# A hybrid decoder layer on one core: the mLSTM memory multiplied at the end, and two decoded rows on shared partitions

## The chip, the core and the metric

The kernel runs on one core of one Trainium2 chip. A core has a matrix engine (PE, with a second track PEld for the loading of its stationary operand), a vector engine (DVE), a scalar engine (ACT), a general engine (POOL) and a queue engine (SP) that issues transfers. ACT and POOL issue transfers as well. SBUF is the core's working memory with 128 partitions; PSUM holds what the matmuls write, in banks of 512 columns of float32.

The metric is the device time of one launch in microseconds, as a median over runs. All times are in microseconds (us) unless marked ns.

## What is computed

One layer of a hybrid decoder is applied to a prompt of 256 tokens and, in the same launch, to 8 single tokens that are being decoded (8 sequences, one new token each). The kernel puts them side by side as 264 columns. In terms of the reference:

```
x = x + W_out[ RGLRU-group(xn) || mLSTM-group(xn) ],  xn = RMSNorm(x)
x = x + CrossAttn(RMSNorm(x), memory K/V)   (4 heads, 256 memory tokens, no mask)
x = x + SwiGLU(RMSNorm(x))
y = RMSNorm_final(x)
```

Two parts matter here.

The mLSTM group has 4 heads with keys of 128 and values of 256. Beside its output, the layer must return each head's memory after the prompt. With the prompt starting from nothing it is one product over the 256 tokens, with a weight `w_end` for each token; the normaliser is the same product with a value of one:

```
C_new = dec[..., None, None] * C + jnp.einsum('bhs,bhsd,bhsv->bhdv', w_end, kc, vc)
n_new = dec[..., None] * n + jnp.einsum('bhs,bhsd->bhd', w_end, kc)
```

Nothing in the layer reads this memory again: it goes to an output (o_pc) and no further.

The cross attention of the 8 decoded rows reads cached keys and values of its own for each row and head, 256 tokens by 512:

```
s = jnp.einsum('blhd,bmhd->bhlm', xq, mk) * (XA_DH ** -0.5)
p = jax.nn.softmax(s, axis=-1)
o = jnp.einsum('bhlm,bmhd->blhd', p, mv)
```

There are 32 such (head, row) pairs, each with 512 KB of keys and 512 KB of values that are used once.

## The kernel before

Activations lie with the feature on the partitions: a [2048, 264] matrix is 16 chunks of [128, 264]. Every weight matrix is cut into pieces of 128 output features by up to 16 input chunks, and the list `steps` holds them in order: w_in (41 pieces), w_out (16), w_q (16), then w_k and w_v for each of the four heads (8 pieces a head), w_o (16), gate and up in three parts, each followed by its w_down pieces. For float32 precision each weight piece is split into a high part (ACT copies it to float32r) and a low part (DVE subtracts), and a product is three matmuls: high by high, high by low, low by high (`mm3`). SP loads the pieces three steps ahead (`load_piece`, line 176) into five buffers `raw`; they are split one step ahead (`split_half`) into four buffers `w`.

The main loop walks over `steps`: it evacuates the step before, splits the next piece, issues the matmuls of this one, loads a later one, and then calls `pump`. Everything that is not a weight matmul is written as a generator (`side`): the recurrent group, the mLSTM group (`ml_prompt`, `ml_values`, `ml_heads`, `ml_sample`, `ml_norm`), the memory's norm (`mem_gen`), the prompt's attention (`attend`), and the decoded rows' attention (`dec_k`, `dec_v`). `pump` runs the generators by their priority until modelled clocks of DVE and ACT have reached PE's, so side work is spread into what DVE and ACT have left in each step. A planner then fixes each engine's order by priorities and a modelled timeline. SP alone keeps the order in which the code is written. Each engine carries out its instructions in order, so one that waits holds up all behind it; POOL's arithmetic and the transfers that it issues are one such order. Nearly all instructions go through a helper and show as line 60 in the profile, so they are told apart by the names of their tiles.

Tiles named B are 26 buffers of about 4 KB per partition that nearly everything in flight shares. PSUM has four banks named mm, for weight matmuls, and four named ax.

The mLSTM heads (`ml_heads`). For head h, `kw` holds the keys times the weight `w_end` with the token on the partitions, two blocks of [128 tokens, 128]; `vt` holds the values with the ones beside them, two blocks of [128, 258]. Two float32 matmuls give the memory in a bank `cps`, ACT copies it into `cn`, and after the fourth head POOL issues one transfer of `cn` to `o_pc` (line 826). Each float32 matmul is two instructions in the profile.

The decoded rows' attention. `dec_k` takes a row: POOL loads keys `kc` (line 1151) and values `vc` (line 1155), each [128, 4, 256]: 512 features on 128 partitions in 4 chunks, by 256 tokens. The scores are summed over the chunks with ACT (first chunk times the query, a column of `qsm`) and DVE (three more multiply-adds) into `acc`, a part of the tile `dw`. ACT and POOL (line 1162) split `acc` into the high and low part `ds`, and in `dec_v` two float32r matmuls with a matrix of ones, `onesr`, sum over the partitions and leave the sum on all of them. DVE takes the maximum, ACT the exponential with its sum in `ssm`, and DVE multiplies each of the 4 chunks of values by the probabilities and sums over the tokens into a column of `osm`. After 8 rows of a head `osm` is divided by `ssm`, and `attend(h)` copies it beside the prompt's columns as input of w_o. At most `NFL` = 2 rows are between `dec_k` and the end of `dec_v`.

The end. In the last part of w_down, `final(m)` adds a piece's result to `xres`, adds its squares to `acc_x`, and scales by the gain into `y`. For the last piece (m = 15) the sum of squares is finished on PE (`fin_sums`), and `rstd_fin` makes the reciprocal root on DVE and ACT and spreads it over partitions by matmuls with `ident`, once into the bank `fin["ps"]` that DVE reads and once into `fin["copied"]`, which ACT copies to `rstd` for POOL. Between these, `warm` issues matmuls whose result nobody reads. Then DVE, and POOL for 4 of the 16 chunks, multiply `y`, and SP and ACT issue nine transfers to `o_y` (line 1495).

## Time and profile before

| | us |
|---|---|
| median of 3 runs | 1456.94 (1456.13 to 1457.64) |
| the profiled execution, own time | 1455.83 |
| its span, first to last instruction | 1454.1 |
| PE busy | 1439.2 (99%) |
| DVE busy | 1045.1 (72%) |
| ACT busy | 794.9 (55%) |
| POOL busy | 128.3 (9%) |
| transfers, mean | 224 GB/s |

The profiled execution is 1.1 below the median, and 1.7 of its time lies outside the span. A line of the groups reads: source line, engine, operation, names written and read, shapes, count, then the busy time of all, the mean ns of one, and the time that the engine sat idle just before them with what ended it. A line of the timeline begins with the start and the length of a merged stretch, both in us. Matmuls are pipelined: the length of one is from its start to its last result, while the next one starts much earlier, so the price of a matmul in a dense row is the distance from its start to the next start. The views by windows give the busy time of each engine in a stretch, then the granted clock of PE, the share of time for which the 16 transfer engines were busy, and the rate.

### The profile page before, as it was taken

Reading aid. Unit: us, or ns where it says so; the run is one execution under the profiler, and the core shown is the slowest. Engines: PE = TensorE matmul, PEld = TensorE weight load, DVE = VectorE, ACT = ScalarE, POOL = GpSimd, SP = SyncE. Lnnn points to the kernel's source line nnn. Section 1 sums busy time; section 2 is a strip of 40 time slices with the busy share of each in tenths; the row PEclk is TensorE's granted clock in tenths of the full one; section 3 lists DMA queues with packets and bytes.
Section 4 is the critical chain, followed back from the end, with each engine's and each line's share of the span. In section 5 each row is a group of like instructions: output and inputs, shape, how many; then the busy total and the mean of one; then the engine's idle time right before and its main releaser. Section 6 shows DMA issues by size and latency. Waiting matters only on the chain.

```text
span 1454.1 us, 30126 instructions
## 1 busy us (share of the span) xinstructions
PE 1439.2 (99%) x12071; PEld 1415.5 (97%) x12071; DVE 1045.1 (72%) x1999; ACT 794.9 (55%) x1279; POOL 128.3 (9%) x204
## 2 busy tenths in 40 slices
PE   9999999999999999999999999999999999999997
PEld 8999999999999999999999999999999999999997
DVE  7966797898899999987675666555665655565564
ACT  7678685666556666655544444434444443444463
POOL 0001210000124343410000000000000000000000
PEclk9999999999999999999999999999999999999999
DMA  9645896557799877955555555555555555555563
GB/s 288 234 171 179 268 363 231 177 178 271 254 344 355 340 284 297 375 172 192 197 195 194 197 193 201 190 202 190 198 194 196 196 198 194 195 197 192 172 195 112
DMA packets 99757, 326.02 MB, mean 224 GB/s; under 512 B 10944, under 2 KB 19824, under 8 KB 99616
## 3 DMA queue, kind: packets, MB, share of 16 engines
q1 hardware_dynamic: 83616, 269.84, 52.8%
q0 software_dynamic: 15136, 53.16, 10.2%
q8 instruction: 94, 1.54, 0.4%
q10 hardware_dynamic: 864, 1.09, 0.2%
q14 instruction: 47, 0.39, 0.1%
HBM read 312.78 MB, written 11.28 MB: 223 GB/s over the span
## 4 chain that ended last, share of the span: by engine, by line
PE 94%; ACT 2%; DMA 1%; DVE 1%; issue 1%; SPq 0%; POOL 0%; DVEq 0%; POOLq 0%
PE mm L60 90%; PE ax L60 5%; DMA raw<-w_in 1%; ACT B L60 1%; DVE B L60 1%; DMA B<-scr 0%; ACT w L60 0%; DVE w L60 0%; ACT L60 0%; SPq L213 0%; ACT dw L60 0%; DVE ds L60 0%; SPq L1412 0%; DMA scr<-lt 0%; ACT t L60 0%
## 5 line engine op out<-in xcount | busy, mean ns | idle before, releaser
L60 PE MATMUL mm<-B,w 128*128 128x264 f32 (+1 forms) x10960 | 1281.2, 279 | 2.5 <-DVE w L60 2.1
L60 PEld LDWEIGHTS mm<-B,w 128*128 128x128 f32 x10960 | 1260.6, 189 | 10.7 <-DVE w L60 2.4
L60 DVE TENSOR_TENSOR w<-raw,w 128x1024 fp32r<-128x1024 f32 (+1 forms) x522 | 625.4, 1200 | 312.9 <-ACT w L60 312.2
L60 ACT ACTIVATE w<-raw 128x1024 fp32r<-128x1024 f32 (+1 forms) x522 | 536.0, 1028 | 531.8 <-PE mm L60 370.8
L60 PE MATMUL mm<-w,B 128*128 128x512 f32 x384 | 86.5, 380 | 0.0
L60 PEld LDWEIGHTS mm<-w,B 128*128 128x128 f32 x384 | 70.7, 189 | 9.4
L1494 POOL TENSOR_TENSOR B<-B,rstd 128x264 f32<-128x264 f32 x4 | 2.8, 741 | 802.8 <-ACT rstd L60 802.8
L60 DVE TENSOR_TENSOR t<-mm,rstd 128x264 f32<-128x264 f32 x96 | 41.4, 432 | 28.8 <-PE mm L60 28.7
L60 DVE SCALAR_TENSOR_TENSOR B<-B,dw 128x256 f32<-128x256 f32 x128 | 52.2, 461 | 3.2 <-ACT dw L60 2.9
L60 DVE TENSOR_TENSOR xres<-xres,mm 128x264 f32<-128x264 f32 (+1 forms) x81 | 34.2, 424 | 27.2 <-PE mm L60 27.1
L60 DVE SCALAR_TENSOR_TENSOR dw<-B,qsm,dw 128x256 f32<-128x256 f32 x96 | 48.6, 512 | 0.8
L60 PE MATMUL ax<-B,B 128*128 128x256 f32 (+3 forms) x288 | 46.0, 302 | 0.8 <-DVE B L60 0.8
L1162 POOL TENSOR_TENSOR ds<-dw,ds 128x256 fp32r<-128x256 f32 x32 | 36.8, 1151 | 106.9 <-ACT ds L60 104.7
L60 PEld LDWEIGHTS ax<-B,B 128*128 128x128 f32 x288 | 39.9, 191 | 3.0 <-DVE B L60 1.0
L60 ACT ACTIVATE B<-xres,vecs 128x264 fp32r<-128x264 f32 (+1 forms) x64 | 32.1, 502 | 3.5 <-DVE xres L60 1.6
L60 ACT ACTIVATE t<-xres 128x264 f32<-128x264 f32 (+1 forms) x53 | 21.0, 409 | 16.0 <-DVE xres L60 16.0
L1151 POOL DMA_DIRECT2D B<-kcT x32 | 17.4, 544 | 122.8 <-DVE B L60 109.7
L60 DVE SCALAR_TENSOR_TENSOR B<-xres,vecs,B 128x264 fp32r<-128x264 f32 x48 | 23.3, 488 | 4.3 <-ACT B L60 4.3
L60 ACT ACTIVATE dw<-B,qsm 128x256 f32<-128x256 f32 x32 | 16.2, 507 | 16.3 <-issue 6.4
L60 ACT ACTIVATE B<-t 128x264 fp32r<-128x264 f32 (+1 forms) x60 | 24.1, 409 | 1.7 <-DVE t L60 1.5
L60 ACT ACTIVATE dw<-B,B 128x128 f32<-128x128 f32 x64 | 20.9, 390 | 7.1 <-DMA B<-scr 6.3
L60 ACT ACTIVATE dw<-ax,dw 128x256 f32<-128x256 f32 x32 | 15.0, 470 | 17.7 <-DVE dw L60 14.0
(172 smaller groups left out, 691.2 us busy)
## 6 DMA issues: line engine op xcount, KB each, us to landing
raw<-w_gu SPq DMA_DIRECT2D x176, 512.0 KB, 3.6
raw<-w_d SPq DMA_DIRECT2D x80, 512.0 KB, 3.7
raw<-w_in SPq DMA_DIRECT2D x74, 512.0 KB, 5.2
raw<-w_out SPq DMA_DIRECT2D x32, 512.0 KB, 3.8
B<-kcT POOLq DMA_DIRECT2D x32, 512.0 KB, 8.2
raw<-w_q SPq DMA_DIRECT2D x32, 512.0 KB, 5.4
B<-vcT POOLq DMA_DIRECT2D x32, 512.0 KB, 9.1
raw<-w_k SPq DMA_DIRECT2D x32, 512.0 KB, 5.1
```

The costliest lines, as they stand in the source:

```text
L60: return f(*a, **k)
L1151: pool_e.dma_start(kc, kcT[h, b])
L1162: pool_e.tensor_sub(ws[:, 1], acc, ws[:, 0].bitcast(F32))
L1494: e.tensor_mul(st["y"](c), st["y"](c), r)
```

## The change

Three things are changed.

First, `ml_heads` no longer multiplies the memory. It writes `kw` and `vt` of each head to DRAM (`kept_k`, `kept_v`; two transfers on POOL's queue a head), and the transfer of `cn` there is gone. In the last part of w_down, at m = 4, `state_load` reads them back on SP's queue into B tiles (`kb` for the keys, two `vb` for the values). The eight float32 matmuls are issued at the end on PE: one in place of two of three `warm` matmuls at m = 15, two in place of the three in `rstd_fin`, one behind the two spreads, and four behind that. ACT copies each head's bank out (`state_out`), and two transfers on SP's queue take the result to `o_pc`: heads 0 and 1 ahead of a transfer of `o_y`, heads 2 and 3 behind the last one. PE keeps the written order in the last step.

Second, the decoded rows' attention takes two rows of one head at once: one on partitions 0 to 63, the other on 64 to 127. A row's 512 features are then 8 chunks of 64. `onesr` becomes block diagonal, so that one pair of matmuls sums both rows apart. Because a row's query and result lie on all 128 partitions elsewhere, `swap_q` brings half of each row's query to the other half of the partitions (POOL copies and two transfers), and `swap_o` brings the results back.

Third, keys and values come through a `Ring` each: two fixed tiles, a tile being half of the features of both rows, filled by two transfers of 64 partitions (256 KB each) and filled again when the four instructions that read it are done.

```diff
@@ -442,11 +442,17 @@
...
         dve.scalar_tensor_tensor(r, t, 1.5, r, op0=OP.add, op1=OP.mult)
-        warm(3, v[:, 0:1])
+        state_mm((0, 1), (1, 0))
         for k in "ps", "copied":
...
             spread(fin[k], [r[:, j: j + 1] for j in range(3)])
+        state_mm((1, 1))
         act.activation(rstd, fin["copied"][:, :N], AF.Copy)
+        state_out(0, act)
+        state_out(1, act)
+        state_mm((2, 0), (2, 1), (3, 0), (3, 1))
+        state_out(2, act)
+        state_out(3, act)
...
@@ -737,6 +743,29 @@
...
     hT = {}
+    kept_k = drm.tile([H, P, T], F32, name="kept_k")
+    kept_v = drm.tile([H, P, 2, 258], F32, name="kept_v")
+    def state_load():
+        kb, vb, out = B([P, H, T]), [B([P, 2, 2, 258]), B([P, 2, 2, 258])], B([P, H, 258])
+        for h in range(H):
+            sp.dma_start(kb[:, h], kept_k[h])
+            sp.dma_start(vb[h // 2][:, h % 2], kept_v[h])
+        fin["state"] = kb, vb, out
+        fin["cps"] = {}
+    def state_mm(*parts):
+        kb, vb, out = fin["state"]
+        for h, t in parts:
+            if t == 0:
+                fin["cps"][h] = bank("ax" if h % 2 else "mm")
+            pe.matmul(fin["cps"][h][:, 0:258], kb[:, h, t * P: t * P + P], vb[h // 2][:, h % 2, t, :],
+                      start=t == 0, stop=t == 1)
+    def state_out(h, engine):
+        out = fin["state"][2]
+        engine.activation(out[:, h, :], fin["cps"][h][:, 0:258], AF.Copy)
...
@@ -796,7 +825,6 @@
...
     def ml_heads():
-        cn = B([P, H, 258])
         hT["t"] = Arr(8)
...
@@ -812,18 +840,15 @@
...
                           start=False, stop=True)
-            cps = bank("ax")
-            pe.matmul(cps[:, 0:258], kw[:, 0:P], vt[:, 0, :], start=True, stop=False)
-            pe.matmul(cps[:, 0:258], kw[:, P:T], vt[:, 1, :], start=False, stop=True)
-            dps = cps[:, 300:302]
+            pool_e.dma_start(kept_k[h], kw)
+            pool_e.dma_start(kept_v[h], vt)
+            dps = bank("ax")[:, 0:2]
             pe.matmul(dps[:, 0:1], Pm[:, 0:P], one, start=True, stop=True)
...
             act.activation(den[:, 3 * h: 3 * h + 2], dps, AF.Abs)
-            act.activation(cn[:, h, :], cps[:, 0:258], AF.Copy)
-        pool_e.dma_start(o_pc, cn)
         yield STEP
...
@@ -1036,7 +1061,8 @@
...
             else:
-                warm(3)
+                state_mm((0, 0))
+                warm(1)
                 sq = tmp()
...
@@ -1047,6 +1073,8 @@
...
                 act.activation(warm_act, acc_x[:, 0:1], AF.Sqrt)
+            elif m == 4:
+                state_load()
             elif m == KC - 2:
...
@@ -1129,70 +1157,131 @@
...
             qn["n"] = j + 1
+            if j % 4 == 3:
+                swap_q(j // 4)
             if j == 3:
                 with tc.issue_after(st["split"].ins):
-                    act.activation(onesr, ones, AF.Copy)
+                    act.activation(onesr, ones, AF.Copy, scale=0.0)
+                    for part in (LOW, HIGH):
+                        act.activation(onesr[part, part], ones[part, part], AF.Copy)
                 st["dk"] = side(dec_k(), 5)
...
     infl = {"n": 0}
+    NB2 = NS // 2
+    q2 = const.tile([P, H, 2, 4, NB2], F32, name="q2")
+    q3 = const.tile([P, H, 4, NB2], F32, name="q3")
+    o2, o3 = q2, q3
+    LOW, HIGH = slice(0, 64), slice(64, P)
+    def rows_of(h, even):
+        return slice(4 * h, 4 * h + 4), slice(0, NS, 2) if even else slice(1, NS, 2)
+    def swap_q(h):
+        for part, even in ((LOW, True), (HIGH, False)):
+            c, b = rows_of(h, even)
+            pool_e.tensor_copy(q2[part, h, 0], qsm[part, c, b])
+            c, b = rows_of(h, not even)
+            pool_e.tensor_copy(q3[part, h], qsm[part, c, b])
+        pool_e.dma_start(q2[LOW, h, 1], q3[HIGH, h])
+        pool_e.dma_start(q2[HIGH, h, 1], q3[LOW, h])
+    def swap_o(h):
+        rec = ssm[:, h, 0: NB2]
+        dve.reciprocal(rec, rec)
+        o = o2[:, h].rearrange("p g c b -> p (g c) b")
+        dve.tensor_mul(o, o, rec.rearrange("p (c b) -> p c b", c=1).to_broadcast([P, 8, NB2]))
+        pool_e.dma_start(o3[LOW, h], o2[HIGH, h, 1])
+        pool_e.dma_start(o3[HIGH, h], o2[LOW, h, 1])
+        for part, even in ((LOW, True), (HIGH, False)):
+            c, b = rows_of(h, even)
+            pool_e.tensor_copy(osm[part, c, b], o2[part, h, 0])
+            c, b = rows_of(h, not even)
+            pool_e.tensor_copy(osm[part, c, b], o3[part, h])
+    class Ring:
+        def __init__(self, src):
+            self.t, self.at = [B([P, 4, T]), B([P, 4, T])], 0
+            self.src = src
+            self.load()
+            self.load()
+        def load(self):
+            u = self.at
+            if u < H * NB2 * 2:
+                self.at = u + 1
+                for q, part in enumerate((LOW, HIGH)):
+                    pool_e.dma_start(self.t[u % 2][part],
+                                     self.src[u // NS, u // 2 % NB2 * 2 + q, HIGH if (u + q) % 2 else LOW])
+        def __call__(self, j):
+            return self.t[j // 4][:, j % 4, :]
     def dec_k():
+        kr = Ring(kcT)
+        st["vr"] = Ring(vcT)
+        yield STEP
         for h in range(H):
...
                 yield STEP
-            for b in range(NS):
+            for b in range(NB2):
                 while infl["n"] >= NFL:
...
                 infl["n"] += 1
-                kc = B([P, 4, T])
-                pool_e.dma_start(kc, kcT[h, b])
                 w = sb.tile([P, 264], F32, tag="dw", bufs=2, name=nm("dw"))
                 ws = sb.tile([P, 2, T], F32R, tag="ds", bufs=2, name=nm("ds"))
-                vc = B([P, 4, T])
-                pool_e.dma_start(vc, vcT[h, b])
                 acc = w[:, 0:T]
-                q = [qsm[:, 4 * h + c, b: b + 1] for c in range(4)]
-                act.activation(acc, kc[:, 0, :], AF.Copy, scale=q[0])
-                for c in range(1, 4):
-                    dve.scalar_tensor_tensor(acc, kc[:, c, :], q[c], acc, op0=OP.mult, op1=OP.add)
+                for j in range(8):
+                    q = q2[:, h, j // 4, j % 4, b: b + 1]
+                    if j == 0:
+                        act.activation(acc, kr(0), AF.Copy, scale=q)
+                    else:
+                        dve.scalar_tensor_tensor(acc, kr(j), q, acc, op0=OP.mult, op1=OP.add)
+                    if j % 4 == 3:
+                        kr.load()
+                    if j == 3:
+                        yield 1.0
                 act.activation(ws[:, 0], acc, AF.Copy)
                 pool_e.tensor_sub(ws[:, 1], acc, ws[:, 0].bitcast(F32))
-                pairs.append((h, b, w, vc, ws))
+                pairs.append((h, b, w, ws))
                 yield 1.1
...
         done, cur = 0, None
-        while done < H * NS:
+        while done < H * NB2:
             nxt = None
...
                 ps = bank("ax")
-                pe.matmul(by2(ps[:, :T]), onesr, turn(nxt[4][:, 0]), start=True, stop=False)
-                pe.matmul(by2(ps[:, :T]), onesr, turn(nxt[4][:, 1]), start=False, stop=True)
+                pe.matmul(by2(ps[:, :T]), onesr, turn(nxt[3][:, 0]), start=True, stop=False)
+                pe.matmul(by2(ps[:, :T]), onesr, turn(nxt[3][:, 1]), start=False, stop=True)
                 nxt += (ps,)
...
                 continue
-            h, b, w, vc, _, ps = todo
+            h, b, w, _, ps = todo
             mx, p = w[:, T: T + 1], w[:, :T]
...
             yield 0.5
-            for c in range(4):
-                dve.scalar_tensor_tensor(vc[:, c, :], vc[:, c, :], 1.0, p, op0=OP.mult, op1=OP.mult,
-                                         accum_out=osm[:, 4 * h + c, b: b + 1])
+            for j in range(8):
+                v = st["vr"](j)
+                dve.scalar_tensor_tensor(v, v, 1.0, p, op0=OP.mult, op1=OP.mult,
+                                         accum_out=o2[:, h, j // 4, j % 4, b: b + 1])
+                if j % 4 == 3:
+                    st["vr"].load()
+                if j == 3:
+                    yield 1.0
             infl["n"] -= 1
             done += 1
-            if done % NS == 0:
-                dve.reciprocal(ssm[:, h, :], ssm[:, h, :])
-                for c in range(4):
-                    dve.tensor_mul(osm[:, 4 * h + c, :], osm[:, 4 * h + c, :], ssm[:, h, :])
+            if done % NB2 == 0:
+                swap_o(h)
+                yield STEP
                 st["dh"] = h + 1
...
@@ -1452,6 +1541,8 @@
...
             pend = []
+        if i == len(steps) - 1:
+            kept.enter_context(tc.manual_schedule(engines={mybir.EngineType.PE}))
         now = pe.clock
...
@@ -1488,11 +1579,15 @@
...
         e(x)
+    kept.close()
     for lo, hi in ((0, 1), (1, 2), (2, 4), (4, 6), (6, 8), (8, 10), (10, 12), (12, 14), (14, 16)):
...
             e.tensor_mul(st["y"](c), st["y"](c), r)
+        if lo == 4:
+            sp.dma_start(o_pc[:, 0:2], fin["state"][2][:, 0:2])
         (act if lo in (1, 4, 8, 12) else sp).dma_start(o_y[:, lo:hi, :], st["y"].tile(lo // 4)[:, lo % 4: lo % 4 + hi - lo, :])
+    sp.dma_start(o_pc[:, 2:4], fin["state"][2][:, 2:4])
...
```

## The prediction

> **What bounds the kernel now.** I read the busy shares first, then PE's groups, then a table by stage, then the timeline of the end.
>
> ```profile
> PE 1439.2 (99%) x12071; PEld 1415.5 (97%) x12071; DVE 1045.1 (72%) x1999; ACT 794.9 (55%) x1279; POOL 128.3 (9%) x204
> L60 PE MATMUL ax<-B,B 128*128 128x258 f32 x16 | 4.2, 388 | 0.8 <-DVE B L60 0.8
> L60 PE MATMUL ax<-ds,onesr 128*128 128x256 f32 x64 | 17.1, 277 | 0.0
> ```
>
> PE is busy for all but 15 us of the span, so a matmul taken out of the middle shortens the run by its price, if nothing else becomes the bound there. The last two rows are those the change touches: 16 instructions of the mLSTM memory and 64 of the decoded rows' sums. Where PE has company is seen by stage.
>
> ```profile
> core 0: us, PE busy (x) PEld busy (x) DVE busy (x) ACT busy (x) POOL busy (x), PEclk, DMA share, GB/s
> 150.00:192.00 42.00, 41.19 (x330) 39.94 (x329) 32.16 (x105) 30.25 (x76) 11.79 (x22) 1.00 0.89 300
> 440.00:640.00 200.00, 200.00 (x1196) 182.96 (x1195) 194.44 (x493) 130.30 (x253) 78.62 (x105) 1.00 0.84 314
> 1300.00:1436.00 136.00, 136.00 (x1211) 136.00 (x1211) 82.25 (x116) 71.10 (x102) 0.00 (x0) 1.00 0.53 176
> ```
>
> From 440 to 640, where the decoded rows run, PE has no gap but DVE is busy for 194.4 of 200 and the transfers for 0.84: three resources are nearly full. From 1300 to 1436 PE alone binds. The end has a chain of its own:
>
> ```profile
> 1441.14 0.58 PE L60 MATMUL mm<-B,w 128*128 128x264 f32 x3
> 1441.56 0.83 PE L60 MATMUL mm<-ones 128*128 128x128 f32 x6
> 1442.45 0.83 PE L60 MATMUL ax<-ones,t 128*128 128x1 f32 x6
> 1443.54 0.94 PE L60 MATMUL mm<-ones,c 128*128 128x128 f32 x6 [0.25 <-DVE c L60]
> 1444.57 1.50 PE L60 MATMUL ax<-ident,c 128*128 128x128 f32 x12
> 1445.45 4.16 DVE L60 TENSOR_TENSOR B<-B,ax 128x264 f32<-128x264 f32 x12 [0.93 <-PE ax L60]
> 1445.90 4.71 SPq L1495 DMA_DIRECT2D o_y<-B  x5
> 1446.12 0.39 ACT L60 ACTIVATE rstd<-ax 128x264 f32<-128x264 f32 x1 [2.39 <-PE ax L60]
> 1446.25 3.22 ACTq L1495 DMA_DIRECT2D o_y<-B  x4
> ```
>
> After the last weight matmul come squares, root, spread, 12 multiplies on DVE and nine transfers. The transfers by themselves, from 1436 to the end (one figure is 0.455 us, the span's last 18.2 in 40):
>
> ```profile
> GB/s 0 0 0 0 0 0 0 0 0 0 0 0 0 0 0 0 0 0 0 0 0 0 0 109 358 174 390 395 385 390 409 385 390 385 390 395 200 0 0 0
> o_y<-B SPq DMA_DIRECT2D x4, 264.0 KB, 2.6
> o_y<-B SPq DMA_DIRECT2D x1, 132.0 KB, 1.8
> ```
>
> From figure 27 on, about 1447.8, the rate stands at 385 to 409 until the last bytes: what is added to this output is paid at that rate, at the very end.
>
> **The change, part by part.** *Memory matmuls out of the middle.* PE starts a head's four instructions and then the next group:
>
> ```profile
> 165.73 1.03 PE L60 MATMUL ax<-B,B 128*128 128x258 f32 x4
> 166.60 0.39 PE L60 MATMUL ax<-ones,B 128*128 128x1 f32 x3
> ```
>
> 166.60 - 165.73 = 0.87 for a head, four heads 3.5 us; the busy time of 4.2 is the upper end, since it counts the tail of the last result. The 0.8 idle before the first is a wait for DVE which the next matmuls inherit. I take -3.5. ACT loses four copies there and POOL one transfer; POOL gains eight for `kept_k` and `kept_v`, in whose way stand the sample's own loads:
>
> ```profile
> L866 POOL DMA_DIRECT2D B<-c0T x8 | 4.3, 536 | 2.5 <-DMA B<-scr 2.1 <-issue 0.3
> L60 ACT ACTIVATE dw<-B,B 128x128 f32<-128x128 f32 x64 | 20.9, 390 | 7.1 <-DMA B<-scr 6.3 <-DVE B L60 0.8
> ```
>
> Eight issues at 0.54 are 4.3 us on POOL, which is busy for 11.8 of 42 there, and 1.57 MB (four heads of 128 x 256 and 128 x 516 float32) are 4.0 us at 390 GB/s where 0.11 of 42, or 4.6, is free. PE hides it with its weights loaded ahead; if that cover fails, the loads come up to 4 us late and take back the gain. I take nothing, with 0 to +3 kept for the range.
>
> *Loading them back.* `state_load` puts eight issues on SP ahead of weight loads at about 1398.
>
> ```profile
> 1397.59 12.48 SPq L176 DMA_DIRECT2D raw<-w_d  x7
> 1399.29 1.06 ACT L60 ACTIVATE w<-raw 128x1024 fp32r<-128x1024 f32 x1 [0.53 <-ACT B L60]
> 1403.34 1.06 ACT L60 ACTIVATE w<-raw 128x1024 fp32r<-128x1024 f32 x1 [0.53 <-ACT B L60]
> raw<-w_d SPq DMA_DIRECT2D x80, 512.0 KB, 3.7
> ```
>
> The splits of two pieces stand 1403.34 - 1399.29 = 4.05 us apart. Five raw buffers are two and a half pieces, so some 10 us lie between an issue and its use; landing takes 3.7. Eight issues, at the 0.53 of POOL's rows at most 4.3, and 4.0 of transfer overlap to about 4: within the 6 that are left. Zero; a late weight would cost up to 2.
>
> *In the end.* On PE the first memory matmul takes the place of two warm ones (0.44 for 0.55) and ends before the squares. The next two, 0.87 by the row above, start after the sums, at about 1443.2, and end near 1444.1: before the root is ready at 1444.57, so the spread is not moved. The rest (five, 2.2 us, until about 1448.3) lies under DVE's multiplies. On ACT four copies, at 0.39 each as `rstd`, come behind `rstd` and, if ACT keeps the written order, ahead of its four transfer issues: the first of these moves from 1446.25 to about 1448.8, the last from 1448.96 to 1449.9. That leaves 132 KB out of the early, unfilled slices (0.3 us). The two new transfers are 528 KB, at 390 GB/s 1.35 us, all of it behind a queue that is already full. Issues end by 1450.6, before the bytes run out. Bounds: 1.0 (the hole at figure 26 filled) to 2.2 (both prices and an issue of 0.53 exposed); I take +1.5.
>
> *Two rows on shared partitions.* PE issues 16 pairs of sums for 32:
>
> ```profile
> 626.72 0.27 PE L60 MATMUL ax<-ds,onesr 128*128 128x256 f32 x1
> 626.83 0.60 PE L60 MATMUL mm<-w,B 128*128 128x512 f32 x2
> ```
>
> 626.83 - 626.72 = 0.11, so 32 fewer are -3.5 us. The other engines:
>
> ```profile
> L60 DVE SCALAR_TENSOR_TENSOR dw<-B,qsm,dw 128x256 f32<-128x256 f32 x96 | 48.6, 512 | 0.8
> L60 DVE TENSOR_REDUCE dw<-ax 128x1 f32<-128x256 f32 x32 | 13.3, 416 | 0.3 <-PE ax L60 0.2
> L60 DVE TENSOR_SCALAR dw<-dw 128x1 f32<-128x1 f32 x32 | 4.7, 147 | 0.2
> L60 ACT ACTIVATE dw<-B,qsm 128x256 f32<-128x256 f32 x32 | 16.2, 507 | 16.3 <-issue 6.4 <-DVE B L60 4.7 <-ACT w L60 2.9
> L1162 POOL TENSOR_TENSOR ds<-dw,ds 128x256 fp32r<-128x256 f32 x32 | 36.8, 1151 | 106.9 <-ACT ds L60 104.7 <-PE mm L60 2.0
> L1151 POOL DMA_DIRECT2D B<-kcT x32 | 17.4, 544 | 122.8 <-DVE B L60 109.7 <-issue 7.1 <-ACT ds L60 3.6
> ```
>
> DVE per pair: one multiply-add more (7 for 6, +0.51), one maximum and one scaling less (-0.56), the eight value multiplies as before; with a shorter division per head about -1 to -2 us in all. ACT loses 16 of its first multiplies and as many copies and exponentials, over 20 us, off the path. POOL loses 16 subtractions (-18) and gains 64 issues (+35) and the swaps (16 issues, 32 small copies: +9 and a few us more); it was busy for 79 of 200, so it does not become the bound, but its queue gets denser. PE's gain is larger than DVE's, and DVE has 5.6 us left in 200: I take the full -3.5, the lower end is 0.
>
> What hides the swap of results is the distance from the last value multiply to its first reader:
>
> ```profile
> 634.31 0.42 DVE L60 SCALAR_TENSOR_TENSOR B<-B,dw 128x256 f32<-128x256 f32 x1
> 647.47 0.49 ACT L60 ACTIVATE B<-osm 128x8 fp32r<-128x8 f32 x4
> ```
>
> 634.7 to 647.5 is 12.8; division, two issues, a landing (1.8 in the smallest row above) and copies are some 5, so 7 to 8 remain for a later end of the decoded rows.
>
> *The sum* against the profiled execution: -3.5 - 3.5 + 1.5 = -5.5, 1455.83 to 1450.3. That execution lies 1.1 under the median of 1456.94, from which the same sum gives 1451.4. I predict 1451.4.
>
> **The rivals.** *The half loads come late (slower).* A ring tile is refilled only when its four readers are done, while before POOL could run several rows ahead.
>
> ```profile
> L60 DVE SCALAR_TENSOR_TENSOR B<-B,dw x128: 403/419/1199, 393.4 to 634.3; 128x256 f32<-128x256 f32 x128
> DMA to landing us min/median/max: 3.8/8.2/13.9
> ```
>
> From 393.4 to 634.7 for 32 rows is 15.1 a pair. Of that the four readers take 2.0 and a weight split (1.2) among them, POOL's subtraction and two issues ahead of the refill 2.2: a landing may take 9.7. The median of the keys' loads is 8.2, the longest 13.9. That is the point from which it decides. At 10.9, 15 pairs are late by 1.2 each, 18 us, of which 8 are hidden as worked out above: 1451.4 + 10 = 1461.4. DVE waits in order with weight splits behind it, so PE would show gaps. For it: DVE is nearly full; against: one load is in flight at a time where before up to four queued up.
>
> *Half the partitions move slower (slower).* The packets of the cached keys and values are on the queue that POOL fills:
>
> ```profile
> q0 software_dynamic: 7565, 26.67, 35.1%
> ```
>
> This is its share from 440 to 640, beside 0.84 for all. If such packets took 1.46 times as long the engines would be full; at 1.6 times the share is 1.05, 10 us too much, and 1451.4 + 3.5 + 10 gives 1465. Doubled, it is 1.19, some 38 us too much. No transfer of this size to 64 partitions is in the trace, so it is open; against it speaks that the weights' packets run between these on the same engines. The Trainium skill is for this rival: the page "SBUF — State Buffer", section "Door 1: The DMA port swizzle (why `[64,N]` ≈ `[32,N]`)", says that a transfer to partitions 0 to 63 reaches only 8 of the 16 ports, and a section further on that two transfers to the two halves serialize. By that rule it would be the doubled case; no run here shows it yet.
>
> *DVE keeps the stage (no change).* If DVE's 194 of 200 is real need, PE's 3.5 there turns into gaps: -3.5 + 1.5, 1454.9.
>
> *The end costs more.* With ACT's issues late and `o_pc` last behind a full queue, +3.5 for 1.5: 1453.4.
>
> **How the numbers follow.** Forecast 0.52 (1448.8 to 1453.9: bounds of the terms), late half loads 0.13, slower half packets 0.11, DVE 0.15, dear end 0.09. Faster or slower than 0.2% is 2.9 us, about what runs of this kernel can tell from no change: below 1454.0, above 1459.9. Faster: forecast, most of the dear end, a little of DVE, 0.62; slower: 0.22 from the two load rivals; same: 0.16. The range from 1448.5 to 1462 leaves out the slow packets and the worst of the late loads.
>
> **What would show it.** The group of 128x258 matmuls lies between 1434 and 1443, PE's last weight matmul ends near 1434.7 instead of 1441.7, and the onesr group counts 32. The table shows PE full from 440 to about 636, with landings of the half loads under 9.7. The output's rate stays near 390 for about 1.4 us longer than before. I am wrong if DVE waits for a ring tile, if POOL's DVE waits move `ds` late, or if PE shows gaps between 381 and 650.

## The result: slower by 3.9%, and the profile after

The changed kernel takes 1514.38 us (median of 5 runs, 1509.39 to 1517.98), the kernel before 1456.94 (5 runs, 1456.13 to 1458.46). The ratio is 1.0392, with a 95% interval from 1.038 to 1.0404. The prediction was 1451.4, and its range ended at 1462. The profiled execution is the quickest of the five, 1509.39 us with a span of 1507.7, so the trace has to explain 53.6 us (1507.7 - 1454.1); the medians lie 57.4 apart, and the rest isn't in it.

The busy times of the changed kernel, and the issues of the loads that feed the decoded rows and of the weights beside them (KB each, then the median us from issue to landing):

```profile
PE 1454.8 (96%) x12029; PEld 1423.4 (94%) x12029; DVE 1043.2 (69%) x1971; ACT 773.1 (51%) x1217; POOL 168.4 (11%) x307
...
raw<-w_k SPq DMA_DIRECT2D x32, 512.0 KB, 10.1
B<-kcT POOLq DMA_DIRECT2D x64, 256.0 KB, 7.6
B<-vcT POOLq DMA_DIRECT2D x64, 256.0 KB, 7.8
```

PE was idle for 15 us of the span before and is idle for 53 now. It also issues 42 matmuls fewer and yet is busy for 15.6 us longer (1439.2 to 1454.8): its matmuls have become slower. DVE and ACT did as the prediction said, 1.9 and 21.8 us less. POOL did 40 more, some 10 above its sum, because the 32 small copies that it put at a few us took 14.4. The groups that the change touches:

```profile
L60 PE MATMUL ax<-ds,onesr 128*128 128x256 f32 x32 | 10.6, 336 | 18.4 <-ACT ds L60 16.3 <-POOL ds L1247 1.8
L60 PE MATMUL mm<-B,B 128*128 128x258 f32 x8 | 2.3, 391 | 0.0
L60 PE MATMUL ax<-B,B 128*128 128x258 f32 x8 | 2.3, 391 | 0.0
L60 DVE SCALAR_TENSOR_TENSOR dw<-B,q,dw 128x256 f32<-128x256 f32 x112 | 57.6, 518 | 33.5 <-DMA B<-kcT 27.1
```

The counts are the announced ones: 32 sums and 16 memory matmuls. New is the idle time in the last column: 18.4 us ahead of the sums, and 27.1 us in which DVE waits for a tile of keys. Where this lies is seen by stage. After the window's length stand the busy times of PE, PEld, DVE, ACT and POOL, then the granted clock, the transfers' share and their rate:

```profile
150.00:192.00 42.00, 39.45 (x314) 38.64 (x313) 29.61 (x87) 26.20 (x62) 13.77 (x25) 0.96 0.88 285
440.00:640.00 200.00, 174.71 (x984) 155.53 (x984) 163.51 (x406) 90.83 (x161) 89.61 (x156) 0.94 1.01 278
460.00:470.00 10.00, 9.90 (x47) 8.98 (x48) 5.32 (x11) 4.14 (x6) 7.12 (x15) 0.73 1.04 273
800.00:1300.00 500.00, 500.00 (x4447) 500.00 (x4446) 290.46 (x340) 215.47 (x247) 0.00 (x0) 1.00 0.59 196
```

From 440 to 640 the changed kernel does 984 matmuls where the one before did 1196. DVE isn't the limit (194.4 busy before, 163.5 now). The transfer engines are: their share is 1.01 for 0.84, and yet they move 278 GB/s for 314. From 800 on PE is full again and nothing more is lost. The waits of that kernel (sum, count, longest, us):

```profile
PE ax L60 <- ACT ds L60: 16.3, 8, 5.2
PE mm L60 <- DVE w L60: 15.6, 8, 6.0
PE ax L60 <- DVE B L60: 2.9, 2, 2.5
...
DVE dw L60 <- DMA B<-kcT: 27.1, 7, 5.5
DVE B L60 <- DMA B<-vcT: 14.2, 5, 5.4
```

DVE stands in 41 us of waits for the two rings of cached keys and values, and PE in some 35 us of waits for what DVE and ACT make. One such place in the timeline:

```profile
525.98 0.42 DVE L60 SCALAR_TENSOR_TENSOR B<-B,dw 128x256 f32<-128x256 f32 x1 [5.43 <-DMA B<-vcT]
...
528.64 1.22 DVE L60 TENSOR_TENSOR w<-raw,w 128x1024 fp32r<-128x1024 f32 x1
529.91 2.50 PE L60 MATMUL mm<-B,w 128*128 128x256 f32 x7 [6.04 <-DVE w L60]
```

DVE works in order. It waits 5.43 us for a tile of values, then does its value multiplies, then splits a weight (528.64 to 529.86), and PE has stood for 6.04 us for just that weight.

How late the kernel is against the one before, by the splits of the same weights: 1.1 us at about 300, 49.4 from 700 to the end (last weight matmuls at 1490.55 for 1441.14). Its tail then takes 1.45 more, and 2.7 more pass at the very end: 49.4 + 1.45 + 2.7 = 53.6. Between 381 and 700 I count on PE 25 gaps of over 250 ns with 39.2 us together (none before). The matmuls between them take 13.0 us longer than at the durations of before, and 3.5 us of sums are gone: 39.2 + 13.0 - 3.5 = 48.7 for the 48.3 us lost there. Most of the 13.0 is the granted clock: by the trace's record of it some 10.8 lie in stretches at half clock, and the rest are gaps under 250 ns. After a gap of 5.2 us that ends at 460.1, the clock over the ten from 460 on is 0.73, and over the stage 0.94. The Trainium skill has this in "TensorE: Matmul & The Clock Gate", section "What's actually happening": PE falls to half its clock after an idle window of about 3.4 us and needs as long of steady work to come back. The trace agrees, with a longer way back: the clock goes to 0.50 at 458.50, 3.6 us into the gap, and is back at 1.00 at 465.33, 5.2 us after its end; the 5.3 us at half clock that lie behind 460 are the 0.73.

Why the engines are full at a lower rate is in the view of the queues from 440 to 640 (packets, MB, share of 16 engines). First the changed kernel, then the one before, whose first queue stands in the prediction:

```profile
q0 software_dynamic: 8439, 26.51, 51.5%
q1 hardware_dynamic: 7922, 28.85, 49.1%
```

```profile
q1 hardware_dynamic: 9854, 35.89, 48.4%
```

The rows' queue, filled by POOL, moves as many bytes as before (26.51 MB for 26.67) but takes 51.5% for 35.1%: a MB costs 1.94% for 1.32%, or 1.48 times as much. The weights' queue, which the change doesn't touch, pays more as well: 1.70% a MB for 1.35%. By the packets of the trace the median time of one of 4 KB goes from 159 ns in both queues to 253 in the rows' and 216 in the weights'.

The end, by the timeline and by the rates from 1490 to 1508 (0.45 us a figure):

```profile
1490.55 0.58 PE L60 MATMUL mm<-B,w 128*128 128x264 f32 x3
1490.97 0.60 PE L60 MATMUL mm<-B,B 128*128 128x258 f32 x2
...
1493.98 1.50 PE L60 MATMUL ax<-ident,c 128*128 128x128 f32 x12 [0.31 <-DVE c L60]
1494.85 4.17 DVE L60 TENSOR_TENSOR B<-B,ax 128x264 f32<-128x264 f32 x12 [0.93 <-PE ax L60]
...
1500.18 1.15 SPq L1590 DMA_DIRECT2D o_pc<-B  x1
```

```profile
GB/s 0 0 0 0 0 18 0 0 0 0 0 0 0 99 350 186 371 381 390 408 385 375 390 404 399 380 380 404 397 285 0 0 0 0 0 0 0 0 0 0
```

The spread starts 3.43 us after the last weight matmuls, as before (1444.57 - 1441.14), so the memory matmuls don't move it. The rate stays at 371 to 408 for three figures longer. From the start of the last weight matmuls to the landing of the last store it is 13.51 us for 12.06: the 1.45 above.

### The profile page after: what moved, and what is told of

Its sections match the earlier page's. It is cut to its first block, busy times and chain, and to the rows that moved or that the text cites. A ratio compares the mean times of both kernels' runs of the same rounds, so it can differ in the third digit from the quotient of the medians.

```text
span 1507.7 us, 30092 instructions
## 1 busy us (share of the span) xinstructions
PE 1454.8 (96%) x12029; PEld 1423.4 (94%) x12029; DVE 1043.2 (69%) x1971; ACT 773.1 (51%) x1217; POOL 168.4 (11%) x307
## 4 chain that ended last, share of the span: by engine, by line
PE 55%; DMA 2%; DVE 1%; issue 0%; ACT 0%; DVEq 0%; POOL 0%; ACTq 0%
PE mm L60 54%; DVE B L60 1%; DMA B<-vcT 1%; PE ax L60 1%; DMA B<-kcT 1%; DVE dw L60 0%; DVE w L60 0%; DVE c L60 0%; DVE t L60 0%; POOL B L1216 0%; DVEq L1674 0%; ACT t L60 0%; DVE xres L60 0%; ACT w L60 0%; ACT c L60 0%
## 5 line engine op out<-in xcount | busy, mean ns | idle before, releaser
L60 PEld LDWEIGHTS mm<-B,w 128*128 128x128 f32 x10960 | 1271.3, 190 | 27.9 <-DVE w L60 15.6
L60 DVE SCALAR_TENSOR_TENSOR dw<-B,q,dw 128x256 f32<-128x256 f32 x112 | 57.6, 518 | 33.5 <-DMA B<-kcT 27.1
L1216 POOL DMA_DIRECT2D B<-kcT x64 | 33.6, 530 | 178.6 <-DVE B L60 95.1
L1216 POOL DMA_DIRECT2D B<-vcT x64 | 33.3, 530 | 48.6 <-DVE B L60 41.2
L60 ACT ACTIVATE dw<-B,q 128x256 f32<-128x256 f32 x16 | 8.2, 510 | 53.7 <-DMA B<-kcT 36.7
L60 PE MATMUL ax<-ds,onesr 128*128 128x256 f32 x32 | 10.6, 336 | 18.4 <-ACT ds L60 16.3
L60 PEld LDWEIGHTS ax<-ds,onesr 128*128 128x128 f32 x32 | 6.4, 203 | 21.9 <-ACT ds L60 19.1
L60 ACT ACTIVATE dw<-B,B 128x128 f32<-128x128 f32 x64 | 20.8, 391 | 12.1 <-DMA B<-scr 10.6
```

The source lines that it names most:

```text
L60: return f(*a, **k)
L1216: pool_e.dma_start(self.t[u % 2][part], self.src[u // NS, u // 2 % NB2 * 2 + q, HIGH if (u + q) % 2 else LOW])
```

## The experiments

The kernel before ran beside each of them, with a median from 1456.4 to 1457.0. Two theories stood for the slow stage: that transfers to 64 partitions are slower on the engines, and that a ring of two tiles brings the loads late at any speed.

### One part at a time

e1 takes the part with the memory alone, e2 the part with the decoded rows alone. What e1 adds to the kernel before, in short:

```diff
-            pe.matmul(cps[:, 0:258], kw[:, 0:P], vt[:, 0, :], start=True, stop=False)
-            pe.matmul(cps[:, 0:258], kw[:, P:T], vt[:, 1, :], start=False, stop=True)
+            pool_e.dma_start(kept_k[h], kw)
+            pool_e.dma_start(kept_v[h], vt)
...
+        if lo == 4:
+            sp.dma_start(o_pc[:, 0:2], fin["state"][2][:, 0:2])
...
+    sp.dma_start(o_pc[:, 2:4], fin["state"][2][:, 2:4])
```

e2 is the rest of the change:

```diff
+    class Ring:
...
+        def load(self):
...
-                kc = B([P, 4, T])
-                pool_e.dma_start(kc, kcT[h, b])
```

> Only the memory part: the eight products at the end, their inputs through DRAM, one transfer order at the end; the decoded rows' attention as before. Theory A (the slower half loads are the cause of all that went wrong): the sum of the prediction without the rows, -3.5 + 1.5 = -2, so 1454 to 1456. Theory B (the writes of the kept inputs on POOL's queue delay the loads of the sample's state): the gain of 3.5 between 150 and 192 us is eaten, as the changed kernel's trace has it (its weight splits are 1.1 us late at 300 us where 3.5 early was forecast), and the end costs about 4 (last weight matmul to the end of the span 12.96 before, 17.15 in the changed kernel), so 1460 to 1463.

> Only the decoded rows' part: two rows on shared partitions, rings, half loads; the memory as before. If the parts add up and the rows carry the loss, the stage from 381 to 700 us costs about 48 more than before (the weight splits of the changed kernel go from 1 us late to 49 late in it): 1503 to 1508. If the memory part's loads at the end or its DRAM writes had a share in the stage, under 1495.

e1 takes 1460.75 us (8 runs, 1457.7 to 1463.02), a ratio of 1.0025 (1.0015 to 1.0036): 3.7 us slower. e2 takes 1510.19 (4 runs), 1.0363 (1.0344 to 1.0381): 53.2 slower. The two together are 56.9, the whole change 57.4, so the parts add up and hardly act on each other. e2 lies above the 1503 to 1508 that were expected: its stage loses the 48 (its weight splits go from 1.3 us late at 381 to 49.3 at 700), and 3.9 more pass at the very end, which the last section takes up. Nearly all of the loss is in the rows, but the memory part is a loss too, where the prediction had -3.5 + 1.5 = -2.0.

### Half loads in the kernel before

e3 is the kernel before with nothing changed but the loads of its cached keys and values: each comes as two transfers of 64 partitions. There is no ring, every row has its own tile and its loads run ahead as before.

```diff
-                pool_e.dma_start(kc, kcT[h, b])
+                for part in (slice(0, 64), slice(64, P)):
+                    pool_e.dma_start(kc[part], kcT[h, b, part])
```

> The kernel before with one thing changed: each load of a row's keys and of its values is cut into two transfers of 64 partitions, same tile, same bytes, same place in the program. Theory A (half-partition packets are slower): the software queue's share per MB between 440 and 640 us rises from 1.32% towards the 1.94% of the changed kernel, the engines fill up and PE starves: 1475 to 1505. Theory C (the shallow ring is the cause, the width of the loads is not): at most 64 more issues of 0.54 us on POOL, which is off the path: within 3 us of 1457.

1512.78 us (4 runs), a ratio of 1.0377 (1.0361 to 1.0392): cutting the loads costs 55.8 us, as much as the whole change and more than the 1475 to 1505 of theory A. Its stage by the windows, its queues there, and the issues with their landings:

```profile
440.00:640.00 200.00, 182.17 (x1042) 163.44 (x1041) 161.58 (x394) 105.27 (x198) 79.07 (x125) 0.96 0.97 273
```

```profile
q0 software_dynamic: 7006, 22.64, 42.5%
q1 hardware_dynamic: 8741, 31.81, 54.0%
```

```profile
B<-kcT POOLq DMA_DIRECT2D x39, 256.0 KB, 12.9
```

A MB costs 1.88% on the rows' queue and 1.70% on the weights', as in the changed kernel. The bytes that the kernel before moves in that stage would cost 26.67 x 1.88 + 35.89 x 1.70 = 111% of it. The landings (12.9 us for 256 KB, where the kernel before has 8.3 for 512 KB in this window) are the queue that this builds up.

One more thing is in e3's trace and not in that of the kernel before. Between 381 and 700 POOL stands still before 56 of its issues until an earlier transfer of its own has landed, 79 us in all. The largest group of these waits:

```profile
POOL B L1152 <- DMA B<-kcT: 34.2, 18, 4.1
```

The program gives POOL's transfers eight semaphores in turn, so no more than eight are on their way, and 42 of these issues start 0.28 us after the transfer eight places ahead has landed. With half loads the eight places hold half the bytes. The subtractions for the sums stand behind these issues in POOL's order, and PE waits 13.9 us for them. So e3 shows that packets of half loads are slower, but what they cost by themselves is not told apart in it from this limit. That takes e5 and e8 below.

### Whole loads in the changed kernel

e4 is the changed kernel with each tile of a ring filled by one transfer of 128 partitions. For this the caches lie in DRAM with two rows interleaved by halves from the start; the ring keeps its two tiles, and the bytes and the arithmetic are the same.

```diff
-                for q, part in enumerate((LOW, HIGH)):
-                    pool_e.dma_start(self.t[u % 2][part],
-                                     self.src[u // NS, u // 2 % NB2 * 2 + q, HIGH if (u + q) % 2 else LOW])
+                pool_e.dma_start(self.t[u % 2], self.src[u // NS, u // 2 % NB2, u % 2])
```

> The changed kernel with the cached keys and values laid out in DRAM by ring tile, so that one transfer of 128 partitions fills a tile; rings as deep as in the changed kernel. Theory A: the share per MB goes back to about 1.32%, the loss of the stage is gone, 1451 to 1462 (what stays is the memory part's own cost). Theory C (a ring of two tiles is refilled too late, whatever the width): 1490 or more, DVE still waiting for transfers of keys and values for over 30 us.

1492.38 us (4 runs), 1.0247 (1.0232 to 1.0262). Packets are back at 159 ns, and still 35 us are lost. The queues of its stage, its DVE wait for keys, the landing of the keys' loads, and a place in its timeline:

```profile
q0 software_dynamic: 7992, 27.41, 39.6%
q1 hardware_dynamic: 8339, 30.36, 43.8%
```

```profile
DVE dw L60 <- DMA B<-kcT: 31.1, 9, 7.8
```

```profile
DMA to landing us min/median/max: 3.6/6.1/8.6
```

```profile
447.30 0.57 POOL L1215 DMA_DIRECT2D B<-kcT  x1 [1.77 <-DVE dw L60]
...
454.38 0.48 DVE L60 SCALAR_TENSOR_TENSOR dw<-B,q,dw 128x256 f32<-128x256 f32 x1 [3.37 <-DMA B<-kcT]
```

Both queues pay 1.44% a MB, and the engines have room (0.84 in all). The keys land in 6.1 us, under the 9.7 that the prediction allowed, and are late nonetheless. The reason, at the place shown, is the order: the planner lets the key multiplies of two pairs follow one another. A tile whose readers are done is refilled by an issue at 447.30, the data is there at 454.3, and DVE had wanted it from 451.0 on. The mean distance of 15.1 us between pairs isn't the distance between a refill and its use.

### Both theories crossed: depth and halves

e5 and e8 are the rows' part alone with four tiles for the keys (two for the values). e5 loads whole tiles as e4 does, e8 loads halves.

```diff
-            self.t, self.at = [B([P, 4, T]), B([P, 4, T])], 0
+            self.t, self.at = [B([P, 4, T]) for _ in range(n)], 0
...
-        kr = Ring(kcT)
-        st["vr"] = Ring(vcT)
+        kr = Ring(kcT, 4)
+        st["vr"] = Ring(vcT, 2)
```

> Only the rows' part, with one transfer of 128 partitions to a ring tile and four tiles instead of two in the keys' ring (values as before, two). The run with whole loads and two tiles still had DVE wait 31 us for keys and was 35 us slower than before. Theory C (the rest of the loss is the keys' ring being refilled too late): DVE's waits for keys fall under 5 us, PE has no gaps from 381 to 640, and the 32 sums that are gone show: 1452 to 1456. Theory D (the two-row form itself is slower, by its POOL swaps or because DVE has no room): 1470 or more with DVE's waits for keys gone.

> Only the rows' part, with the half loads of the change but four tiles in the keys' ring. Theory A (half packets take about 250 ns instead of 159, so the engines are full whatever the depth): share of the engines still 0.95 or more, 1490 to 1510. Theory C alone (depth is all that matters): 1452 to 1465.

e5 takes 1463.38 us (4 runs), 1.0053 (1.0036 to 1.0069). e8 takes 1512.16 (4 runs), 1.0383 (1.0367 to 1.0398). Depth takes away most of the loss when the loads are whole (e5 against e4, which also has the memory part, 3.7 us in e1), and nothing when they are halves (e8 against e2). In e8's stage the engines are as full as in the changed kernel, and the wait has only moved from the keys to the values, which still have two tiles; its window, its queue and its DVE wait:

```profile
440.00:640.00 200.00, 172.66 (x963) 154.03 (x963) 155.97 (x392) 90.77 (x159) 91.08 (x147) 0.94 1.02 276
```

```profile
q0 software_dynamic: 8225, 25.62, 51.2%
```

```profile
DVE B L60 <- DMA B<-vcT: 44.6, 13, 8.0
```

e5 and e8 differ in the loads alone (and in the order in DRAM that whole loads need), and e8 is 48.8 us slower, some 4 of them at the very end. POOL's issues of keys and values wait only 2.2 us for earlier landings in e8 between 381 and 700, and only 0.5 us of PE's waits end with POOL, so here it is the slower packets. The two causes are separate, and each is enough to lose over 30 us: halves with either ring (e2 53, e8 55), and the short ring with whole loads (e4 35). They don't add; in both the same readers wait.

### What was left of the rows' part

e5 still loses 6.4 us. Its timeline shows one place that costs PE 2.46:

```profile
572.20 0.69 POOL L1174 COPY osm<-q 64x16 f32<-64x16 f32 x1 [4.70 <-DMA q<-q]
...
575.36 0.78 POOL L1217 TENSOR_TENSOR ds<-dw,ds 128x256 fp32r<-128x256 f32 x1
576.20 0.38 PE L60 MATMUL ax<-ds,onesr 128*128 128x256 f32 x1 [2.46 <-POOL ds L1217]
```

POOL waits 4.70 us for the swap of a head's results (the landings of all swaps, of queries and results, take 3.2 to 9.2, the median 5.4) before it may copy them. The subtraction that PE's sums need is behind this copy in POOL's order. e9 is e5 with these copies emitted two steps later; e10 is e9 with the subtraction on DVE.

```diff
+    def swap_back(h):
...
+                for _ in range(2):
+                    yield STEP
+                swap_back(h)
```

```diff
-                pool_e.tensor_sub(ws[:, 1], acc, ws[:, 0].bitcast(F32))
+                dve.tensor_sub(ws[:, 1], acc, ws[:, 0].bitcast(F32))
```

> The rows' part with whole loads and four tiles in the keys' ring (6.4 us slower than before, PE with six gaps of 6.7 us together that end with POOL's low part of a sum), and the copies that bring the results back to their own half written two steps later than the transfers that they wait for. Theory F (POOL stands still for these transfers, 4.7 us at 567.5 us, with the subtraction behind it that PE waits for): POOL's waits for them fall under 2 us, the gaps near 511 and 573 us go, 1456 to 1460. Theory G (it is the refills, waiting for DVE on POOL's queue, that hold the subtraction up): 1462 to 1465, gaps as many as before.

> As the run with the copies later, and the 16 subtractions that make the low part moved from POOL to DVE, so nothing that PE waits for stands in POOL's queue; DVE gains 16 times 0.42, 6.7 us, of the 12.4 it had idle between 440 and 640. Theories F and G both say that PE's waits for POOL are gone: 1453 to 1457, faster than before by up to the 3.5 of the sums. Theory H (DVE then is the bound): PE waits for weight splits instead, 1457 to 1465.

e9 takes 1459.68 us (10 runs), 1.0019 (1.001 to 1.0029), and e10 1458.12 (10 runs), 1.0004 (0.9994 to 1.0013). PE's wait for the subtraction goes from 3.9 us in e5 to 0.3 in e9, whose other waits are named here, and then e10's:

```profile
PE ax L60 <- POOL ds L1219: 0.3, 1, 0.3
PE ax L60 <- DVE B L60: 3.6, 4, 1.5
```

```profile
PE mm L60 <- DVE w L60: 5.3, 5, 1.9
```

Theory F's other sign did not come: in e9 POOL still waits 9.9 us for the swaps (11.5 in e5), so two steps later is not late enough. The subtraction is in time nonetheless, and what of the new order brings that about was not separated; theory G is not excluded. e10's waits are those of theory H, and its interval overlaps that of e9.

With everything mended the rows' part is as fast as before and no faster: the 3.5 us of sums that PE no longer does are paid back in small gaps. Between 381 and 700 PE waits 4.1 us in e10, 3.3 of them for DVE, and not at all in the kernel before (of the 5.3 in the row above 2.9 lie there). Whether DVE has to be that late or the planner's order makes it so wasn't tried.

### The memory part with another issuer

e6 is e1 with the eight transfers that keep the inputs issued by ACT; e12 is the same kernel again.

```diff
-            pool_e.dma_start(kept_k[h], kw)
-            pool_e.dma_start(kept_v[h], vt)
+            act.dma_start(kept_k[h], kw)
+            act.dma_start(kept_v[h], vt)
```

> Only the memory part, with the eight writes of the kept inputs issued by ACT, which made these inputs, instead of POOL. Theory B (on POOL's queue the writes hold up the loads of the sample's state, and PE waits for what comes from them): weight splits at 300 us about 3.5 early instead of 0.3, PE's waits for DVE back to those of before, and with 1.4 us more of transfers at the end 1454 to 1456. Theory E (the bytes themselves crowd the transfer engines between 150 and 192 us, wherever they are issued): as the memory part alone, 1458 to 1462.

> The memory part alone with the writes on ACT's queue, as it ran before, timed in more rounds: 1454 to 1456 if its gain of 1.8 is real, 1457 if it was the chip's.

e6 takes 1455.16 us (10 runs), 0.9989 (0.998 to 0.9999); e12 takes 1454.83 (11 runs), 0.999 (0.9981 to 0.9999). Moving eight issues from one queue to another is worth 5 to 6 us against e1. The timeline of the mLSTM stage in the kernel before, in e1 and in e6:

```profile
151.63 1.08 POOL L870 DMA_DIRECT2D B<-scr  x2
...
161.00 1.28 ACT L60 ACTIVATE dw<-B,B 128x128 f32<-128x128 f32 x4 [0.81 <-DMA B<-scr]
```

```profile
155.62 0.56 POOL L843 DMA_DIRECT2D kept_k<-B  x1 [3.20 <-ACT B L60]
156.70 1.10 POOL L895 DMA_DIRECT2D B<-scr  x2
...
165.08 1.28 ACT L60 ACTIVATE dw<-B,B 128x128 f32<-128x128 f32 x4 [4.26 <-DMA B<-scr]
167.94 0.83 PE L60 MATMUL ax<-ones,B 128*128 128x1 f32 x6 [2.28 <-DVE B L60]
```

```profile
152.45 1.08 POOL L895 DMA_DIRECT2D B<-scr  x2
...
162.26 1.28 ACT L60 ACTIVATE dw<-B,B 128x128 f32<-128x128 f32 x4 [0.52 <-DMA B<-scr]
```

In e1 the issue of `kept_k` waits 3.20 us for ACT's product, and the loads from `scr` stand behind it on POOL: they leave at 156.70 for 151.63. ACT needs them 4.26 us before they come, DVE waits for ACT, and PE stands for 2.28 for what DVE makes. With ACT as the issuer a transfer follows its own producer and waits for nothing; the `scr` loads leave at 152.45. At about 300 us e6 is 2.8 us ahead of the kernel before and e1 0.3, which is 2.5 of the difference. The profiled execution of e1 is its quickest, 1457.7, so its trace doesn't show where its other runs spend 3 us more; that stays open.

### Both parts, mended

e7 has both parts with whole loads, four tiles of keys and ACT's issues. e11 adds the late copies and the subtraction on DVE.

```diff
+            act.dma_start(kept_k[h], kw)
+            act.dma_start(kept_v[h], vt)
...
+        kr = Ring(kcT, 4)
+        st["vr"] = Ring(vcT, 2)
...
+                dve.tensor_sub(ws[:, 1], acc, ws[:, 0].bitcast(F32))
...
+                swap_back(h)
```

> Both parts, with whole loads, four tiles in the keys' ring and the kept inputs' writes issued by ACT. If the parts add up and theories A, B and C hold: the forecast of the prediction, 1450 to 1454, faster than before. If one of them falls, the sum of what the two single runs beside it show.

> Both parts with all that was mended: whole loads, four tiles in the keys' ring, the copies back two steps later, the subtraction on DVE, the kept inputs written by ACT. If the parts add up: the memory part's -1.8 and the rows' +1.3 give 1456 to 1457, no change that can be told. If they disturb each other (the memory part moves the planner's order in the decoded rows' stage), 1458 or more.

e7 takes 1461.99 us (5 runs), 1.0035 (1.0022 to 1.0048), and e11 1456.89 (11 runs), 1.0002 (0.9993 to 1.0011). e7 misses the 1450 to 1454, but it is what its parts give: +6.4 (e5) and -1.8 (e6) make +4.6, and +5.0 was measured. From the 57.4 us of the change all is won back to within the interval, and nothing beyond. The quickest of all kernels here is the memory part alone with ACT's issues, 0.1% under the kernel before in both of its comparisons.

## Why the prediction was wrong

**Half loads.** The step that failed is that the sum has no term for the loads to half the partitions. It lets their bytes cost what whole loads cost, and leaves the rest to the rival "half the partitions move slower" with a chance of 0.11. The runs showed 1.48 times the engine time for a MB of them, 1.26 times for the weights' (1.70% for 1.35%), and 48.8 us between e5 and e8. The rival's mechanism was right, and so was the point from which it decides: packets 1.46 times as long would fill the engines, and with 1.48 the share was 1.01. No price in the prediction came near 1514.4; the highest was this rival's 1465. The page that spoke for it (the Trainium skill, "SBUF — State Buffer", "Door 1: The DMA port swizzle (why `[64,N]` ≈ `[32,N]`)") has such a transfer reach half of the ports; the trace agrees in direction, with packets of 253 ns for 159, and not with the doubling that I drew from it. The rates that the same section gives for transfers of 1 MiB, 196 GB/s to 64 partitions and 328 to 128, are a factor of 1.67 and nearer to it. What I held against it, that the weights' packets run between these on the same engines, turned out the other way round: those packets became slower as well (216 ns). For this reason the price of the rival was too low too. I let 10 us of transfer excess stand for the loss. By the measured shares the stage's bytes need 26.67 x 1.94 + 35.89 x 1.70 = 113% of the 200 us, 25 us too much from 440 to 640 alone, and the gaps cost more than their length, since the granted clock fell after them (most of the 13.0 us between 381 and 700).

**The ring.** "The half loads come late" was right that a tile refilled after its readers comes late; the step that failed is the budget of 9.7 us for a landing, taken from a mean pitch of 15.1 us a pair. e4 landed in 6.1 us at the median, 8.6 at most, and lost 35 us, because two pairs' multiplies follow one another. Its price, 10 us, was a third of that.

**POOL's queue past the kept writes.** I named the loads that stand behind the eight issues and then took nothing for them, with 0 to +3 for the range. It was +3.2 in e1's trace (-0.3 at 300 us for the -3.5 of the matmuls) and +4.6 in the changed kernel's (+1.1). I priced the issues by their 0.54 us each. What cost the time in e1 was the wait of the first write of keys for its producer (3.20 us), which the queue passed on to the loads behind it. (The bytes kept are 1.58 MB, where the prediction has 1.57; nothing hangs on it.)

**The memory matmuls out of the middle.** -3.5 was forecast, and -2.8 was seen in e6 and -2.1 in e12, the same kernel, where the writes are out of POOL's way; what lies between wasn't followed further. Loading them back was forecast at zero and is zero: the lateness is the same 49.4 us from 700 on and at the last weight matmuls, behind the eight issues.

**The end.** +1.5 was forecast, +1.45 measured, with the spread unmoved as worked out. The bytes are most of it (1.35); the delay of ACT's issues was not there, the first left at 1495.65, or 1446.24 with the lateness of 49.41 taken off, for 1446.25 before. So that half of the working was wrong and cost little. The rival of the dear end falls. In the changed kernel 2.7 us more than before pass after the landing of the last store, which no step had; see below.

**The sums and DVE.** The 32 sums left PE's work at the price forecast: 39.2 + 13.0 - 3.5 is 48.7 for a measured 48.3, and the same sum for e4 (27.8 + 10.6 - 3.5 = 34.9 for 34.4) fits as well. As time they were never won: e10 stands at 1.0004. In that the rival "DVE keeps the stage", no gain from the sums, came nearest, though DVE is busy for less than before in every kernel with the rows' part (1039.6 to 1043.2 us for 1045.1). DVE's own work was sized rightly, -1.9 for -1 to -2.

**The swap of results.** I let a landing take the 1.8 us of the smallest row and found 7 to 8 us to spare. Under the load of the stage the median was 5.4 (e5), and the copies that wait for it stood in POOL's order ahead of a subtraction on which PE waits. e9, with these copies later, wins 3.7 of e5's 6.4 us (1463.38 to 1459.68); PE's wait for the subtraction (3.9 to 0.3) speaks for POOL's wait for the swaps as the cause, and POOL's own waits, which hardly fell, don't show it. Here, too, I had looked at who reads the result and not at what is queued behind the wait.

## What to carry to other kernels

Where the transfer engines are as busy as here (0.84), a load cut into two halves by partitions isn't free though its bytes and packets are the same: multiply its queue's share by the 1.5 measured here, raise the others' by a quarter, and see whether the sum passes 1. Count the places in flight too: a load in two halves takes two of the program's eight. A ring's budget is the shortest distance between a tile's last reader and its next first one in the order that is really played, not the mean. And a transfer that has to wait for its producer is better issued by the engine that produces its data: on POOL's queue all that stood behind it waited as well, and that was 5 to 6 us here.

## What the runs showed of the hardware beyond this

- Transfers to 64 partitions slow those to 128 beside them: the weights' packets of 4 KB took 209 to 225 ns in the kernels with halves (changed kernel, e2, e3, e8: 216, 209, 225, 224) and 159 in those without (before, e1, e4, e5, e6). Which resource the two share wasn't tried.
- Gaps on PE cost more than their length: with 39.2 us of gaps over 250 ns came 13.0 us of longer matmuls and short gaps in the changed kernel, with 38.4 came 14.7 in e3, with 27.8 came 10.6 in e4, with 6.7 came 3.5 in e5. Of these some 10.8, 12.7, 7.2 and 1.7 lie in stretches at half clock.
- After its last multiply POOL has a DRAIN record, and on the whole this ends the later the more transfers POOL has issued: 1.97 us after the multiply with 130 (e6, e12), 2.05 with 131 (before), 2.87 with 147 (e5, e9, e10), 3.77 with 154 (e4; but e1's 138 already have 2.87), 6.13 with 195 (e3), 7.44 with 211 (e2, e8) and 8.02 with 218 (the changed kernel). In the kernels with half loads POOL goes on until 2.3 to 3.9 us after SP has seen the last store land (2.4 in the changed kernel, 3.9 in e2, 2.3 in e3, 3.6 in e8), and the span ends with it; with whole loads the DRAIN ends before that. No kernel with that many whole transfers was run, so their form isn't excluded.
